# Gate and up projections of a two-layer encoder by Strassen's seven products, gated values kept as float32

## The chip, the cores and the metric

The kernel runs on one core of a Trainium2 chip, in one launch. The metric is the device time of the whole program in microseconds, the median of several executions. The core's engines are TensorE (PE in the rows: matmuls, with weight loads, PEld, beside them), VectorE (DVE), ScalarE (ACT), GpSimd (POOL) and SyncE (SP), whose queue issues all of the large transfers.

## The reference

Two layers over 512 tokens of width 1024, all in float32. Each layer first mixes positions (differential attention, grouped-query attention and a gated MLP over positions, from one input projection, then an output projection and a layer norm) and then applies the FFN that the change is about:

```python
x = layer_norm(ALPHA * x + mix(x), g1, b1)
gate, up = x @ w_gate, x @ w_up          # 1024 -> 2816 each
x = layer_norm(ALPHA * x + (silu(gate) * up) @ w_down, g2, b2)
```

2816 hidden columns are 22 tiles of 128, called j here.

## The kernel before

Every float32 operand is split into a high part (a cast to the matmul's format, on ScalarE) and a low part (the value minus the cast, on VectorE); `put` (L192 to L195) issues the two. `mm` (L183) then issues three matmuls into one accumulator: high by high, high by low, low by high.

Weights come in pieces of 128 x 1024 float32 (512 KB). `prefetch` walks one list of pieces in the order of use, loads a piece into a raw buffer by a transfer on SyncE, and puts it into two slots of RING (eight slots of 1024 columns, high and low) as soon as two are free; `done` gives slots back. So SyncE's transfers, ScalarE's casts and VectorE's subtractions of the weights run ahead of TensorE as far as slots allow.

The FFN of a layer starts in `main` after the output projection w_out. Per block of 128 tokens (tb) w_out's second half ends with `residual` and `layer_norm` (L298 to L314), and `turn_x` transposes the block's 1024 columns in two banks of PSUM and puts them into xT: two splits of 512 columns per block, of which block 3's are the last.

`gate_up` then runs per tile j: a gate and an up matrix, each 8 slices of 128 of the contraction, each slice `mm` on 512 tokens: 2 x 8 x 3 = 48 matmuls of 512 columns. Tiles 0 and 1 are done in two halves of 256 tokens, the first half while blocks 2 and 3 are still in the output projection's layer norm. `hidden` (L811 to L816) takes silu of the gate on ScalarE, the product with up on VectorE, and puts it into hT, split for the next product. `down` multiplies hT by w_dn, with 22 pieces; its first 16 tiles run in order, the last six (`ntail`) are kept for a pass block by block, so that the layer norms of blocks 0 to 2 lie under TensorE.

GpSimd computes only the layer norms' power (`rsqrt`, L235) in this part. An order within each engine's queue is chosen at build time by a scheduler that follows the program order and the priorities in `PRI`; TensorE's order is that of the generators in `Flow`.

## Time and profile before

| | |
|---|---|
| median of 3 runs | 1199.77 us (1199.49 to 1199.92) |
| profiled execution, its own span | 1198.6 us |
| TensorE busy | 1174.0 us, 98% |
| VectorE busy | 634.3 us, 53% |
| ScalarE busy | 497.5 us, 42% |
| GpSimd busy | 127.6 us, 11% |
| layer 0, gate and up, tiles 0 and 1 in halves | 233.6 to 262.2 us |
| layer 0, gate and up, tiles 2 to 21 | 262.2 to 479.8 us |
| layer 0, down | 479.8 to 599.7 us |
| granted TensorE clock, all 40 slices of the page | 0.9 or more |

The profile covers one execution, so its span is compared with itself and the medians with each other. Times in the timeline are counted from the start of the span. A busy share is a mean over stages: the windows show each stage on its own, and the idle time behind a group of instructions names the engine or the transfer that ended the wait.

### The profile page before, as it was taken

How to read it: one execution, taken by the hardware profiler on the slowest of the kernel's cores; microseconds unless marked ns; L12 is line 12 of the kernel's file. 1: busy time of each engine (PE TensorE's matmuls, PEld its weight loads, DVE VectorE, ACT ScalarE, POOL GpSimd, SP SyncE). 2: the span in 40 equal slices, each digit the busy share in tenths (PEclk: the TensorE clock that was granted, in tenths of full speed). 3: DMA queues.
4: the chain of work that ended last, by engine and by line, in shares of the span. 5: the costliest groups of instructions: out<-in, count | busy, mean ns of one | idle time of the engine just before them, and what ended most of it. 6: DMA issues, size and time to landing. Idle time of an engine off the chain costs nothing.

```text
span 1198.6 us, 14610 instructions
## 1 busy us (share of the span) xinstructions
PE 1174.0 (98%) x5634; PEld 941.8 (79%) x5634; DVE 634.3 (53%) x1084; ACT 497.5 (42%) x1000; POOL 127.6 (11%) x118
## 2 busy tenths in 40 slices
PE   9999989999999999999999999999999999999997
PEld 7787666798888888888878776677988888888886
DVE  5788977843332334230774889788333333333316
ACT  5678856433232323220154788663322232332200
POOL 1233230100000000000231232301000000000001
PEclk9999999999999999999999999999999999999999
DMA  8302130042323233441051022202323232234301
GB/s 290 136 1 89 57 103 1 27 168 88 106 88 106 88 106 106 137 145 53 1 164 52 18 71 85 74 1 84 128 90 103 90 104 93 101 106 151 112 1 71
DMA packets 32757, 107.64 MB, mean 90 GB/s; under 512 B 4656, under 2 KB 5680, under 8 KB 32688
## 3 DMA queue, kind: packets, MB, share of 16 engines
q1 hardware_dynamic: 32688, 106.71, 27.1%
q8 instruction: 44, 0.72, 0.3%
q14 instruction: 25, 0.20, 0.0%
HBM read 104.60 MB, written 2.10 MB: 89 GB/s over the span
## 4 chain that ended last, share of the span: by engine, by line
PE 85%; DVE 8%; issue 2%; ACT 2%; DMA 1%; POOL 1%; POOLq 0%; ACTq 0%
PE bank L78 81%; PE bank L82 5%; DMA RAW<-w_in 1%; POOL st L235 1%; DVE XT L195 1%; DVE st L638 1%; DVE we L753 1%; DVE st L743 1%; DVE qTB L611 0%; DVE we L644 0%; DVE X L314 0%; DVE st L302 0%; DVE X L300 0%; POOL RING L209 0%; DVE RING L195 0%
## 5 line engine op out<-in xcount | busy, mean ns | idle before, releaser
L78 PE MATMUL bank<-XT,RING 128*128 128x512 f32 (+1 forms) x2304 | 484.6, 372 | 0.4 <-DVE RING L195 0.4
L78 PEld LDWEIGHTS bank<-XT,RING 128*128 128x128 f32 x2304 | 407.8, 188 | 75.6 <-DVE RING L195 0.9
L194 ACT CAST RING<-RAW 128x1024 fp32r<-128x1024 f32 (+1 forms) x138 | 143.6, 1041 | 399.2 <-PE bank L78 355.0
L195 DVE TENSOR_TENSOR RING<-RAW,RING 128x1024 fp32r<-128x1024 f32 (+1 forms) x130 | 157.1, 1209 | 199.0 <-ACT RING L194 194.6
L78 PE MATMUL bank<-RING,XT 128*128 128x512 f32 x576 | 158.7, 405 | 0.5 <-DVE XT L195 0.3
L235 POOL TENSOR_TENSOR st<-st 128x1 f32<-128x1 f32 (+2 forms) x44 | 54.1, 1230 | 665.4 <-DVE st L308 531.3
L78 PEld LDWEIGHTS bank<-RING,XT 128*128 128x128 f32 x576 | 106.0, 189 | 23.2 <-ACT RING L194 0.7
L815 DVE TENSOR_TENSOR sg<-sg,bank 128x512 f32<-128x512 f32 x44 | 30.3, 688 | 137.1 <-PE bank L78 135.7
L82 PE MATMUL bank<-ident,we 128*128 128x128 f32 x400 | 62.1, 274 | 6.6 <-DVE va L704 5.0
L82 PEld LDWEIGHTS bank<-ident,we 128*128 128x128 f32 x400 | 48.4, 140 | 23.2 <-ACT XT L194 4.0
L750 ACT ACTIVATE we<-bank,st 128x512 f32<-128x512 f32 x64 | 50.6, 791 | 17.8 <-DVE st L746 16.6
L300 DVE SCALAR_TENSOR_TENSOR X<-X,bank 128x512 f32<-128x512 f32 x32 | 21.9, 683 | 66.9 <-PE bank L78 66.8
L78 PE MATMUL bank<-XT,mixAC 128*128 128x512 f32 x192 | 54.8, 413 | 0.7 <-DVE XT L195 0.7
L743 DVE TENSOR_REDUCE st<-bank 128x1 f32<-128x512 f32 x64 | 43.7, 685 | 14.8 <-PE bank L78 14.2
L639 ACT ACTIVATE we<-bank,st 128x512 f32<-128x512 f32 x64 | 44.3, 698 | 13.0 <-DVE st L638 8.8
L725 ACT COPY we<-bank 128x512 f32<-128x512 f32 x64 | 37.8, 591 | 23.1 <-PE bank L82 23.0
L638 DVE TENSOR_REDUCE st<-bank 128x1 f32<-128x512 f32 x64 | 43.3, 682 | 5.1 <-PE bank L78 4.8
L78 PE MATMUL bank<-kT,qTB 128*128 128x512 f32 x128 | 44.4, 428 | 0.7 <-ACT we L750 0.7
L78 PE MATMUL bank<-we,va 128*64 128x512 f32 x192 | 43.8, 598 | 0.0
L78 PEld LDWEIGHTS bank<-XT,mixAC 128*128 128x128 f32 x192 | 35.6, 194 | 9.0 <-DVE XT L195 1.2
L78 PE MATMUL bank<-RING,mixBr1a 128*128 128x512 f32 x128 | 42.7, 411 | 0.0
L209 POOL TENSOR_TENSOR RING<-RAW,RING 128x512 fp32r<-128x512 f32 x4 | 7.1, 1781 | 311.2 <-ACT RING L207 311.2
(178 smaller groups left out, 1548.8 us busy)
## 6 DMA issues: line engine op xcount, KB each, us to landing
RAW<-w_gu SPq DMA_DIRECT2D x88, 512.0 KB, 3.5
RAW<-w_dn SPq DMA_DIRECT2D x44, 512.0 KB, 3.5
RAW<-w_in SPq DMA_DIRECT2D x28, 512.0 KB, 3.6
RAW<-w_out SPq DMA_DIRECT2D x16, 512.0 KB, 3.6
we<-xT SPq DMA_DIRECT2D x8, 256.0 KB, 5.3
X<-x SPq DMA_DIRECT2D x4, 512.0 KB, 7.1
GB<-ln_g SPq DMA_DIRECT2D x4, 512.0 KB, 4.9
GB<-ln_b SPq DMA_DIRECT2D x4, 512.0 KB, 4.6
```

Source lines behind the costliest of these rows:

```text
L78: self.pin(self.nc.tensor.matmul(out, lhs, rhs, **kw))
L82: self.pin(self.nc.tensor.transpose(out, src, ident))
L194: nc.scalar.copy(out=r(dst[0]), in_=src)
L195: (low or nc.vector).tensor_tensor(out=r(dst[1]), in0=src, in1=dst[0], op=ALU.subtract)
L235: POOL.tensor_tensor(out=out, in0=src, in1=k.mhalf[:, 0:n], op=ALU.pow)
L300: DVE.scalar_tensor_tensor(out=xs, in0=xs, scalar=scale, in1=bank, op0=ALU.mult, op1=ALU.add)
L638: DVE.tensor_reduce(out=nm, in_=S, op=ALU.max, axis=AX.X, negate=True)
L639: ACT.activation(out=e[m], in_=S, func=AF.Exp, bias=nm, accum_out=ss[m])
L725: ACT.copy(out=wT[:, :, c], in_=tbk.rearrange("p (k q) -> p k q", k=NT))
L743: DVE.tensor_reduce(out=nm, in_=S, op=ALU.max, axis=AX.X, negate=True)
L750: ACT.activation(out=p_, in_=S, func=AF.Exp, bias=nb, scale=sc, accum_out=s_)
L815: DVE.tensor_tensor(out=sg, in0=sg, in1=B[bk[1]], op=ALU.mult)
```

## The change

Tokens are cut into two halves (0 to 255, 256 to 511) and the contraction into two halves of 512. With these and the two column blocks gate and up, each tile is a product of 2 x 2 blocks, and Strassen's form (in Winograd's variant) computes it by seven products instead of eight. A product is 4 slices x 3 matmuls of 256 columns, 12 matmuls. `gate_up` runs two tiles at a time, product by product in turn, in the order 1, 7, 6, 2, 5, 4, 3.

The operands are sums. On the token side, `turn_xs` takes for blocks 0 and 1 the two splits as before and a raw copy; for each of blocks 2 and 3 it makes four sums of 512 columns on VectorE and five splits, into seven arrays `blk`. On the weight side, `operand_gu` makes four differences of 128 x 512 per tile on GpSimd; each product's operand is then put into one ring slot, so that eight products can be ahead. The raw weights of a tile are four buffers in rotation.

Products 1 and 2 need only blocks 0 and 1 of the tokens and unchanged gate weights. For the first six tiles (`NEARLY`) they run first, twelve products, with weights loaded for them alone (the gate piece of these tiles is loaded again for the rest). The other products are 10 per pair of tiles for tiles 0 to 5 and 14 for the rest.

`gates` joins the products: sums that share a bank are accumulated there, and between them ScalarE or VectorE copies a bank into another one, or into `m7`, `up2` or `hid`. For a tile of the first six, product 1 is kept in `hid` and copied back into a bank by VectorE before product 6. GpSimd multiplies one half of the gated values (128 x 256), VectorE the other. `hid` stays float32, and is put into slots ("hd" in the list of pieces) in the down stage, beside w_dn; the last six tiles' go where raw weights were. w_out's second half is used in the order 6, 7, 4, 5, and pieces 4 and 5 go where xT was.

```diff
+NEARLY = 6
+PRODUCTS = [(j, i) for n in range(0, NEARLY, 2) for i in (1, 2) for j in (n, n + 1)]
+PRODUCTS += [(j, i) for n in range(0, NF, 2) for i in (1, 7, 6, 2, 5, 4, 3) for j in (n, n + 1)
+             if n >= NEARLY or i not in (1, 2)]
...
+        def diff(n, out, x, y):
+            if n not in t:
+                with pri("wsum"):
+                    ins = POOL.tensor_tensor(out=out, in0=x, in1=y, op=ALU.subtract)
...
+        if i in (1, 2, 3):
+            return (g0, g1, u1)[i - 1]
+        t7 = diff(7, k.wt7[j % 4], u1, u0)
...
+        t5 = diff(5, u0, u0, g0)
...
+        t6 = diff(6, g0, u1, t5)
+        return t6 if i == 6 else diff(4, g1, g1, t6)
...
-            pool_ = spare if key[0] == "dn" and len(spare) >= NS else free
...
+            pools = [more, free] if key[0] in ("gu", "hd", "dn") and pool_ is free else [pool_]
...
+                if n == 1:
+                    parts = [s[0][:, 0:T], s[0][:, T:2 * T]]
+                    k.put(parts, operand_gu(*key[1:]) if key[0] == "gu" else k.hid[key[2]])
...
+            if tb >= 2:
+                with pri("turn_x"):
+                    r22, s1, s2, s3 = (flat(t) for t in k.xsum[tb - 2])
+                    a11, a12 = (k.rawA[i][:, :, cols] for i in range(2))
+                    DVE.tensor_tensor(out=s3, in0=a11, in1=src[0], op=ALU.subtract)
+                    ACT.copy(out=r22, in_=src[1])
+                    k.put(part(7), s3)
+                    DVE.tensor_tensor(out=s1, in0=src[0], in1=r22, op=ALU.add)
+                    DVE.tensor_tensor(out=s2, in0=s1, in1=a11, op=ALU.subtract)
+                    k.put(part(6), s2)
+                    k.put(part(5), s1)
+                    k.put(part(4), src[1])
+                    DVE.tensor_tensor(out=r22, in0=a12, in1=s2, op=ALU.subtract)
+                    k.put(part(3), r22)
...
+        def product(j, i, bank, start):
+            w = need(("gu", l, j, i))
+            for kk in range(4):
+                k.mm(bank[:, HT[0]], [q[:, kk * P:(kk + 1) * P] for q in w], [x[:, kk] for x in k.blk[i]],
+                     start and kk == 0, kk == 3, skip_group_check=True)
...
+                if i == 1:
+                    if j < NEARLY:
+                        ACT.copy(out=h2, in_=p)
+                    else:
+                        ACT.copy(out=q, in_=p)
+                elif i == 2:
+                    ACT.activation(out=h1, in_=p, func=AF.Silu)
+                elif i == 7:
+                    ACT.copy(out=m7, in_=v)
+                    if j < NEARLY:
+                        DVE.tensor_copy(out=q, in_=h2)
+                elif i == 6:
+                    ACT.copy(out=v, in_=q)
+                elif i == 5:
+                    DVE.tensor_tensor(out=up2, in0=v, in1=m7, op=ALU.add)
+                elif i == 4:
+                    DVE.tensor_tensor(out=h2, in0=q, in1=m7, op=ALU.add)
+                    ACT.activation(out=h2, in_=h2, func=AF.Silu)
+                    POOL.tensor_tensor(out=h2, in0=h2, in1=up2, op=ALU.mult)
+                elif i == 3:
+                    DVE.tensor_tensor(out=h1, in0=h1, in1=v, op=ALU.mult)
```

How this moves instructions, at three places of layer 0. In the program's rows L93 is a matmul and L97 a transpose of after (L78 and L82 before), L249 and L250 the cast and the subtraction of `put` (L194 and L195 before), L433 and L434 the layer norm's last two steps (L313 and L314 before), L345 a weight difference.

TensorE before, from the end of w_out into the FFN (`bank_69`, `70`, `74` and `75` hold tiles 0 and 1; `bank_72` and `73` take the transposes of blocks 2 and 3):

```order
L78 MATMUL bank_70<-RING,mixBr1b_1382 128x512
L78 MATMUL bank_69<-XT,RING 128x256
L82 MATMUL bank_72<-ident,X 128x128
L78 MATMUL bank_69<-XT,RING 128x256
L82 MATMUL bank_72<-ident,X 128x128 x3
L78 MATMUL bank_69<-XT,RING 128x256 x11
L78 MATMUL bank_70<-XT,RING 128x256
L82 MATMUL bank_73<-ident,X 128x128 x4
L78 MATMUL bank_69<-XT,RING 128x256 x11
L78 MATMUL bank_70<-XT,RING 128x256 x23
```

and after, from the fifth of the twelve early products to product 6 of tiles 0 and 1 (`blkr` holds token sums):

```order
L97 MATMUL bank_71<-ident,X 128x128 x4
L93 MATMUL bank_74<-XT,RING 128x256 x12
L97 MATMUL bank_76<-ident,X 128x128 x4
...
L93 MATMUL bank_74<-XT,RING 128x256 x12
L93 MATMUL bank_75<-XT,RING 128x256 x12
L93 MATMUL bank_72<-blkr_1598,RING 128x256 x12
L93 MATMUL bank_73<-blkr_1598,RING 128x256 x12
L93 MATMUL bank_69<-blkr_1598,RING 128x256 x12
L93 MATMUL bank_70<-blkr_1598,RING 128x256 x12
```

The twelve early products, in banks 74 and 75 in turn, and products 7 of both tiles stand ahead of product 6 of tile 0, the first into `bank_69`.

VectorE before, from the last layer norm of w_out (block 3) into the first gates:

```order
L313 SCALAR_TENSOR_TENSOR X<-X,st,GB 128x1024
L195 TENSOR_TENSOR RING<-RAW,RING 128x1024 [waits DMAHW5_49,Activation_49]
L314 SCALAR_TENSOR_TENSOR X<-X,st,GB 128x1024 [waits DVE_49,Pool_49]
L195 TENSOR_TENSOR XT<-bank_73,XT 128x4x128 [waits PE_49]
L195 TENSOR_TENSOR RING<-RAW,RING 128x1024 [waits DMAHW6_49,Activation_49]
L195 TENSOR_TENSOR XT<-bank_72,XT 128x4x128 [waits Activation_49]
L195 TENSOR_TENSOR XT<-bank_73,XT 128x4x128 [waits Activation_49]
L195 TENSOR_TENSOR RING<-RAW,RING 128x1024 [waits DMAHW0_49,PE_49,Activation_49]
L815 TENSOR_TENSOR sg_1931<-sg_1931,bank_70 128x512 [waits PE_49,Activation_49]
```

and after, the head and the end of what stands between the same layer norm and the copies of product 1 back into banks 69 and 70 (`xsum` are the token sums, `ffnwe` raw weights and their differences, `ffnqk` is `hid`):

```order
L434 SCALAR_TENSOR_TENSOR X<-X,st,GB 128x1024 [waits DVE_49,Pool_49]
L947 TENSOR_TENSOR xsumkT_1914<-blkraw_1600,bank_72 128x512 [waits PE_49]
L950 TENSOR_TENSOR xsumkT_1914<-bank_72,xsumkT_1914 128x512 [waits Activation_49]
L250 TENSOR_TENSOR RING<-RAW,RING 128x512 [waits DMAHW3_49,PE_49,Activation_49]
L250 TENSOR_TENSOR blkr_1598<-xsumkT_1914,blkr_1598 128x4x128 [waits Activation_49]
L951 TENSOR_TENSOR xsumkT_1914<-xsumkT_1914,blkraw_1600 128x512 [waits DVE_49]
...
L250 TENSOR_TENSOR blkq_1599<-xsumva_1915,blkq_1599 128x4x128 [waits Activation_49]
L250 TENSOR_TENSOR RING<-ffnwe_1823,RING 128x512 [waits DMAHW2_49,PE_49]
L250 TENSOR_TENSOR RING<-ffnwe_1823,RING 128x512 [waits PE_49,Pool_49]
L250 TENSOR_TENSOR RING<-ffnwe_1823,RING 128x512 [waits PE_49,Activation_49] x3
L987 COPY bank_69<-ffnqk_1958 128x256
L987 COPY bank_70<-ffnqk_1958 128x256
```

Between L434 of block 3 and the first L987 stand 32 operations of 512 columns: six that read a bank, 26 with two SBUF inputs.

GpSimd before, from the layer norms of w_out (L235) to those of the layer's end:

```order
L195 TENSOR_TENSOR RING<-RAW,RING 128x1024 x4
L235 TENSOR_TENSOR st<-st 128x1 x4
L209 TENSOR_TENSOR RING<-RAW,RING 128x512
L235 TENSOR_TENSOR st<-st 128x1 x3
L209 TENSOR_TENSOR RING<-RAW,RING 128x512 x3
```

and after, from the same layer norms (now L290) on (`ffnw` is the fourth raw buffer, L995 the multiplication):

```order
L290 TENSOR_TENSOR st<-st 128x1 x4
L345 TENSOR_TENSOR ffnwe_1823<-ffnwe_1823 128x512 x8
L345 TENSOR_TENSOR ffnwe_1823<-RAW 128x512
L345 TENSOR_TENSOR RAW<-RAW 128x512 x3
L345 TENSOR_TENSOR ffnwe_1823<-ffnw_2176 128x512
L345 TENSOR_TENSOR ffnw_2176<-ffnw_2176 128x512 x3
L345 TENSOR_TENSOR ffnwe_1823<-ffnwe_1823 128x512 x8
L995 TENSOR_TENSOR ffnqk_1958<-ffnqk_1958,ffnr1b_2175 128x256 x2
L345 TENSOR_TENSOR ffnwe_1823<-RAW 128x512
```

GpSimd's queue, which held nothing in the FFN but the layer norms, now holds eight differences per pair of tiles (tiles 0 to 5 ahead of the first multiplication).

## Rows read from the trace of the kernel before

**Rows 1.** The page, part 1: engine, busy us, share of the span, instructions.

```profile
PE 1174.0 (98%) x5634; PEld 941.8 (79%) x5634; DVE 634.3 (53%) x1084; ACT 497.5 (42%) x1000; POOL 127.6 (11%) x118
```

**Rows 2.** Windows of layer 0's FFN (columns in its first line).

```profile
core 0: us, PE busy (x) PEld busy (x) DVE busy (x) ACT busy (x) POOL busy (x), PEclk, DMA share, GB/s
233.60:245.00 11.40, 11.19 (x94) 10.95 (x93) 9.96 (x14) 4.42 (x7) 1.52 (x1) 1.00 0.53 179
...
262.20:479.80 217.60, 217.60 (x961) 180.23 (x961) 75.94 (x81) 64.62 (x81) 0.00 (x0) 1.00 0.31 100
479.80:599.70 119.90, 119.90 (x531) 97.58 (x530) 43.51 (x50) 23.15 (x24) 8.41 (x6) 1.00 0.26 84
```

**Rows 3.** Chain of waits, 233 to 340: start, us, what.

```profile
236.77 6.60 PE bank L78 x55
243.83 0.11 PE bank L82
...
245.33 94.84 PE bank L78 x472
```

**Rows 4.** Lines by form, whole run; behind the bar busy us, mean ns.

```profile
L78 PEld LDWEIGHTS bank<-XT,RING 128*128 128x128 f32 x2304 | 407.8, 188 | 75.6 <-DVE RING L195 0.9
L195 DVE TENSOR_TENSOR RING<-RAW,RING 128x1024 fp32r<-128x1024 f32 x126 | 154.3, 1225 | 198.3 <-ACT RING L194 193.9
L194 ACT CAST RING<-RAW 128x1024 fp32r<-128x1024 f32 x134 | 141.1, 1053 | 398.2 <-PE bank L78 355.0 <-DMA RAW<-w_dn 27.8 <-DMA RAW<-w_gu 6.8
L194 ACT CAST RING<-RAW 128x512 fp32r<-128x512 f32 x4 | 2.5, 621 | 1.0 <-DMA RAW<-w_in 0.8
L479 DVE TENSOR_TENSOR rope<-bank,tabs 128x256 f32<-128x256 f32 x16 | 5.9, 412 | 0.8 <-POOL rope L480 0.8
L561 POOL TENSOR_TENSOR GB<-tabs,GB 128x256 f32<-128x256 f32 x4 | 2.9, 735 | 6.7 <-PE bank L78 6.5
```

**Rows 5.** Timeline of GpSimd and VectorE, 27 to 32.6: start, us, engine line op.

```profile
27.33 1.29 POOL L480 TENSOR_TENSOR rope<-rope 128x512 f32<-128x512 f32 x1 [5.50 <-DVE rope L479]
29.49 2.21 POOL L480 TENSOR_TENSOR rope<-rope 128x512 f32<-128x512 f32 x1 [0.87 <-DVE rope L479]
29.33 1.21 DVE L195 TENSOR_TENSOR earlyva<-RAW,earlyva 128x1024 fp32r<-128x1024 f32 x1
30.46 2.38 DVE L352 TENSOR_TENSOR nat<-rope,nat 128x512 fp32r<-128x512 f32 x2
```

**Rows 6.** Timeline of the same two engines at the end of layer 0.

```profile
597.61 0.69 DVE L209 TENSOR_TENSOR RING<-RAW,RING 128x512 fp32r<-128x512 f32 x1
598.56 1.46 DVE L209 TENSOR_TENSOR RING<-RAW,RING 128x512 fp32r<-128x512 f32 x1 [0.26 <-ACT RING L207]
597.66 3.50 POOL L209 TENSOR_TENSOR RING<-RAW,RING 128x512 fp32r<-128x512 f32 x2 [3.44 <-ACT RING L207]
```

**Rows 7.** Timeline of VectorE and GpSimd at the FFN's start.

```profile
238.32 1.52 POOL L235 TENSOR_TENSOR st<-st 128x1 f32<-128x1 f32 x1 [7.54 <-DVE st L308]
240.50 1.28 DVE L314 SCALAR_TENSOR_TENSOR X<-X,st,GB 128x1024 f32<-128x1024 f32 x1
241.69 0.68 DVE L195 TENSOR_TENSOR XT<-bank,XT 128x512 fp32r<-128x512 f32 x1
242.29 1.21 DVE L195 TENSOR_TENSOR RING<-RAW,RING 128x1024 fp32r<-128x1024 f32 x1
```

**Rows 8.** TensorE after a rest: its timeline, and the window behind it.

```profile
159.03 0.63 PE L82 MATMUL bank<-ident,rope 128*128 128x128 f32 x4 [3.08 <-ACT we L725]
160.20:163.60 3.40, 3.40 (x10) 2.63 (x9) 2.07 (x3) 2.66 (x4) 2.30 (x1) 0.50 0.08 25
```

**Rows 9.** Timeline of TensorE where layer 1 begins.

```profile
601.01 0.73 PE L78 MATMUL bank<-RING,XT 128*128 128x512 f32 x2 [0.24 <-ACT XT L194]
```

More of the change, by code (lines that the diff above doesn't have):

```diff
@@ L289, in done @@
     def done(key):
-        _, s, pool_ = held.pop(key)
-        if pool_ is spare or pool_ is free:
-            pool_.extend(s)
+        _, s, homes = held.pop(key)
+        for b, x in zip(s, homes):
+            if x is free or x is more:
+                x.append(b)
         prefetch()
@@ L337, in build @@
             s = [free.pop(0) for _ in range(NS)]
[L338 removed]
+            held[key] = (s, s, [free] * NS)
             nxt[0] += 1
@@ new lines, in turn_xs @@
+        def turn_xs(tb, banks, name):
+            yield LAT["ln"]
+            if tb == 2:
+                yield ev("pv b", NT - 1)
+                k.start_sums(l)
+            cols = slice((tb % 2) * P, (tb % 2 + 1) * P)
+            part = lambda i: [a[:, :, cols] for a in k.blk[i]]
+            flat = lambda t: t.rearrange("p (c t) -> p c t", c=4)
+            src = [flat(banks[hf]) for hf in range(2)]
+            for hf in range(2):
+                with pri("turn_x"):
+                    transposes(banks[hf], lambda c: X[:, tb, (hf * 4 + c) * P:(hf * 4 + c + 1) * P])
+                    if tb < 2:
+                        ACT.copy(out=k.rawA[hf][:, :, cols], in_=src[hf])
+                        k.put(part(1 + hf), src[hf])
+                if hf == 0:
+                    yield 0.0
+            if tb >= 2:
+                with pri("turn_x"):
+                    r22, s1, s2, s3 = (flat(t) for t in k.xsum[tb - 2])
[10 more added lines that the diff above has]
+                    k.put(part(3), r22)
+            F.mark(name, LAT["put"])
@@ new lines, in gate_up @@
+        def gate_up():
+            k.start_ffn(l)
+            got = 0
+            for j, i in PRODUCTS:
+                while got < 4 and not (j < NEARLY and i in (1, 2) and got >= 2):
+                    yield ev("y", got)
+                    got += 1
+                    if got == 4:
+                        k.start_ffn2(l)
+                        k.start_weights2(l)
+                        ready["weights"] = (l, 2)
+                        prefetch()
+                if j < NEARLY and i in (1, 2):
+                    p = (5, 6)[j % 2]
+                else:
+                    p = ((5, 6), (2, 7))[j // 2 % 2][j % 2]
+                bk = (p, (0, 1)[j % 2], (3, 4)[j % 2])
+                bank = B[bk[{1: 0, 2: 0, 6: 1, 4: 1, 7: 2, 5: 2, 3: 2}[i]]]
+                yield from product(j, i, bank, i in (1, 7))
+                gates(j, i, bank, bk)
+                yield 0.0
+            for tag in ("qk1q", "qk1k"):
+                more.extend(k.slots(tag, f"slot{tag}{l}", 2))
+            hfree.extend(k.slots("we", f"slotw{l}", 6))
+            prefetch()
@@ L828, in ffn @@
-            yield ev("y", 1)
-            for j in range(2):
-                yield from gate_up(j, pairs[j % 4], early)
-            yield ev("y", 2)
-            yield ev("y", 3)
-            for j in range(2):
-                yield from gate_up(j, pairs[j % 4], late)
-                hidden(j, pairs[j % 4])
-            for j in range(2, NF):
-                yield from gate_up(j, pairs[j % 4], slice(0, T))
-                hidden(j, pairs[j % 4])
-            dbank = [pairs[(NF - 4 + i) % 4] for i in range(4)]
@@ L867, in ffn @@
                         done(("dn", l, j))
-                    spare.clear()
+                        held.pop(("hd", l, j))
+                    more.clear()
+                    hfree.clear()
                 with pri("ln"):
```

182 lines of the change are left out of this document (131 added, 51 removed).

## The prediction

> **What bounds the kernel now.** I read the page's busy shares first, then the stages of one layer's FFN, then the chain of waits, then prices by line and form, and last single windows in which VectorE and GpSimd work at once. TensorE is busy for 1174.0 of 1198.6 us [rows 1], and in the gate and up stage it never rests: from 262.2 to 479.8, twenty tiles of 48 matmuls, 217.60 of 217.60 us [rows 2], 10.88 us per tile or 0.2267 per matmul of 512 columns. The chain there is TensorE alone [rows 3], where a 256-column matmul takes 6.60/55 = 0.120 us. Beside it VectorE works 75.94 us, ScalarE 64.62 and GpSimd nothing [rows 2]. So a matmul taken away is time taken away, as long as the other engines keep up with what is put on them.
>
> **Products removed: the gain.** Per layer the two first tiles, in halves, cost 2 x 96 x 0.120 = 23.04 us and the other twenty 217.60, together 240.64. After, 22 tiles of 7 products of 12 matmuls of 256 columns are 22 x 84 x 0.120 = 221.76. The gain is 18.88 per layer, **37.8 us** for both. The 256-column pace already stands in the trace with one weight load per matmul, so that the doubled number of loads per column is in the price.
>
> **Work added in the steady state (pairs 3 to 10).** A pair of tiles is 28 x 6 x 0.120 = 20.16 us of TensorE. In this time GpSimd has 8 subtractions of 128x512 and 2 multiplications of 128x256, VectorE 14 low parts of 512 columns and 6 gate steps of 256, ScalarE 14 casts and about 10 copies and silus. ScalarE: 14 x 0.62 + 10 x 0.4 = 12.7, covered [rows 4]. GpSimd alone: 8 x 1.29 [rows 5] + 2 x 0.73 [rows 4] = 11.8, covered. VectorE alone: 14 x 0.60 (start to start, 241.69 to 242.29 [rows 7]) + 6 x 0.41 [rows 4] = 10.9, covered. But the two don't run beside each other where both read SBUF. At 29.49 a GpSimd sum takes 2.21 instead of 1.29: VectorE had begun a two-input SBUF subtraction at 29.33 that held until 30.54, and GpSimd ended 31.70 - 30.54 = 1.16 later; VectorE's next pair took 2.38 instead of 1.29, and its first ended 0.54 after GpSimd's end [rows 5]. At 597.66 two GpSimd subtractions beside such work take 3.50, 1.75 each [rows 6]. So an alternation costs 1.15 + 0.60, one after the other. At 27.33 GpSimd needs its lone 1.29 [rows 5].
>
> The six gate steps have one input in PSUM; I count them as free to run beside GpSimd. What excludes each other in a pair is then 8 x 1.15 + 2 x 0.6 + 14 x 0.60 = 18.8 us, 93% of 20.16. I take a loss of 0, with the ring of eight converted products (8 x 1.44 = 11.5 us of TensorE) against jitter. If the six steps are blocked too it is 18.8 + 2.5 = 21.3, a loss of 1.1 per pair. Between 0 and 9 per layer for eight pairs.
>
> The Trainium skill, in "SBUF — State Buffer" (section "🔬 SBUF: two separate sides"), says that VectorE with two SBUF inputs and a GpSimd operation that reads SBUF exclude each other for the whole instruction, whichever starts first. It speaks against a change that puts 88 subtractions per layer on GpSimd beside 154 of VectorE's; the 2.21 us row agrees with it. By its wording the gate steps, with one PSUM input, aren't held, which is the 0 above; without that distinction the price would be the 9.
>
> **Pairs 0 to 2.** Here 10 products per pair are left, 14.4 us, against 10.4 + 10 x 0.60 = 16.4 of shared reading: 2.0 short each, 6 per layer if nothing was done ahead, 0 if the full ring and the GpSimd results made during the wait described next cover it. I take **2 per layer**.
>
> **The front: the new wait.** Before, each block of 128 tokens was turned with two splits of 512 columns. Now blocks 2 and 3 each need four sums and five splits, and product 6 of tile 0 waits for a VectorE copy that reloads its bank from `hid`; it is queued behind 32 VectorE operations of 512 columns that follow the last layer norm. TensorE's side: it starts at 233.6 [rows 2], has 12 early products, 7(0) and 7(1) in front, 14 x 1.44 = 20.16, and 16 transposes of 0.11 [rows 3]: product 6(0) could start at 255.5. VectorE's side: the last normalisation ends at 240.50 + 1.28 = 241.78 [rows 7]; 32 x 0.60 = 19.2, and the copy 0.41: 261.4 with GpSimd silent. GpSimd begins after its rsqrt, 238.32 + 1.52 = 239.84 [rows 7], with the eight subtractions of tiles 0 and 1: 8 x 1.15 = 9.2. Six of the 32 take one input from PSUM and can hide at most 3.6 of it; I take 2.5, since GpSimd isn't always running when they come. 241.78 + 19.2 + 9.2 - 2.5 + 0.41 = 268.1, a wait of **12.6 per layer**, between 5.9 (no exclusion) and 15.1 (nothing hidden). Waits of single early products on ScalarE, whose queue holds the split of block 2's second sum ahead of a bank's silu, lie inside this time: they delay TensorE, but VectorE's queue ends later. What is queued behind the copy is the next puts; they have slots to spare only after it.
>
> TensorE's old rest at the start of the stage, 11.40 - 11.19 = 0.2 us per layer [rows 2], is within the new wait: I subtract 0.4 for both.
>
> **The clock.** TensorE at 159.03 had rested 3.08 us, and from 160.2 to 163.6 the granted clock was 0.50, 1.2 GHz instead of 2.4 [rows 8]: 3.4 us at half pace, 1.7 lost. Inside the front such a drop is hidden by VectorE's lateness; after the last wait it is not. Between 0 and 1.7 per layer; I take **1**.
>
> **Layer change, once.** The last six pieces of w_dn now hold all the ring until the last block, so that w_in's first pieces of layer 1 are split afterwards: a cast of 1.05 and a subtraction of 1.23 [rows 4] where TensorE now resumes at 601.01 after 0.24 us [rows 9]. Between 0 and 4 (four pieces, one after another, partly under matmuls); I take **2**.
>
> **Edits with one answer.** Six gate pieces per layer are loaded twice, 12 x 512 KB: the DMA share in the stage is 0.31 [rows 2], hidden. `hid` is split in the down stage instead of at the gates: the same cast and subtraction, under a stage in which VectorE works 43.51 of 119.90 us [rows 2]. w_out's rows in the order 6, 7, 4, 5 wait for XT: 0 to 1 per layer, 0 taken, the stage's VectorE is busiest there.
>
> **Sum.** -37.8 + 2 x 12.6 - 0.4 + 2 x 2 + 2 x 1 + 2 = -5.0 us. The profiled span is 1198.6 and the median of the runs 1199.77, 1.2 more that lies outside the span and stays: 1199.8 - 5.0 = **1194.8**.
>
> **Rivals.** *Cover holds (B).* The exclusion costs little in the front because GpSimd finds gaps while VectorE waits for transposes and casts: the wait is 5.9, pairs 0 to 2 lose nothing, the clock stays. -37.8 + 11.8 - 0.4 + 2 = -24.4, **1175**. For it: VectorE's queue does stand still for ScalarE at several places; against: both queues are full at exactly 240 to 268, and the rows show no sharing. *The shared read is the bound (C), slower.* The gate steps are held as well, 21.3 per pair: 9 per layer, the front 15.1, pairs 0 to 2 some 4, together 28 per layer: -37.8 + 56.4 - 0.4 + 2 + 2 = +22.2, **1222** at full price. Its place is GpSimd's subtraction beside VectorE's split, and it decides from (37.8 + 0.4 - 4) / 2 = 17.1 us of loss per layer on. For it: 93% is near the end of what can be hidden; against: a pair can use the time TensorE waits in the front to get ahead. *The products don't run at 0.120 (D)*, because loads of 188 ns [rows 4] show through: nothing in rows 3, with the same shapes, says so. At 0.140 per matmul it would be 22 x 84 x 0.020 = 37 per layer more, far slower.
>
> **How the numbers follow.** A as summed 0.47 (1184 to 1203), B 0.25 (1172 to 1184), C 0.25 (1203 to 1222), D 0.03. A measurement of this kernel tells 0.2%, 2.4 us, from no change. Faster by over that (below 1197.4): all of B and 0.33 of A, 0.58. Within: 0.14, the upper part of A. Slower: C and D, 0.28. The range leaves out the lowest of B and the upper half of C with D: 1174 to 1212.
>
> **What would show it.** The stretch of 14-product pairs should show TensorE starting a tile every 10.08 us without rests. The front should show the VectorE copy into a bank near 268 and TensorE waiting for it; if that wait is under 7 us, B; if over 14, or if TensorE waits for VectorE's RING in every pair, C. GpSimd's subtraction should average 1.7 us beside VectorE, and VectorE's put about 1.2 where it meets one. A granted clock of 0.50 after 6(0) confirms the clock's term. Wrong would be: other waits at the head, above all ScalarE's queue standing for VectorE's sums longer than the copy does, or down-stage splits that come late.

## The result: slower by 1.1%, and the profile after

The changed kernel takes 1213.5 us (median of 4 runs, 1210.9 to 1215.3) against 1199.9 before; the ratio is 1.0108 (95% interval 1.0087 to 1.013). The forecast was 1194.8, the range 1174 to 1212. The profiled span grew from 1198.6 to 1210.7 us. One run of e4_wout_order below, 1615.8 us at a granted clock of 0.65, is left out of its time. These are two lines of the page after: busy time, share and instructions of each engine, and the shares of the chain that ended last ("issue" is time for which the profile shows no cause).

```profile
PE 1153.9 (95%) x7026; PEld 985.6 (81%) x7026; DVE 890.7 (74%) x1432; ACT 633.7 (52%) x1420; POOL 439.8 (36%) x338
...
PE 60%; DVE 13%; issue 11%; POOL 8%; ACT 4%; DMA 4%; SPq 0%; POOLq 0%; DVEq 0%; ACTq 0%
```

TensorE's busy time went down by 20 us and its idle time up by 32. GpSimd went from 127.6 to 439.8 us and VectorE from 634.3 to 890.7 (before: [rows 1]). In the chain of the whole run VectorE, GpSimd and "issue" now hold 32%, 11% before; in this stage TensorE then stood alone in the chain ([rows 3]).

TensorE's waits by what ended them (total us, times, longest). L979 is ScalarE's copy of product 1 out of its bank, L987 VectorE's copy back, L997 the last gate step of a tile:

```profile
PE bank L93 <- ACT ffnqk L979: 12.7, 4, 3.9
PE bank L93 <- DVE bank L987: 9.9, 2, 5.3
...
PE bank L93 <- DVE ffnva L997: 1.8, 4, 0.6
PE bank L93 <- DVE ffnkT L997: 1.5, 4, 0.5
PE bank L93 <- DVE ffnr1a L997: 1.0, 2, 0.6
PE bank L93 <- DVE ffnqk L997: 0.8, 2, 0.5
```

12.7 + 9.9 us are the front of both layers, 5.1 us the places between pairs of tiles. These are idle times at one instruction each; what the stage lost in all is in the table below. First the front of layer 0: start, us, engine, line and what released it, for TensorE, GpSimd, ScalarE and VectorE.

```profile
246.41 2.93 PE L93 MATMUL bank<-XT,RING 128*128 128x256 f32 x12 [2.85 <-ACT ffnqk L979]
252.46 9.17 PE L93 MATMUL bank<-XT,RING 128*128 128x256 f32 x60 [3.12 <-ACT ffnqk L979]
...
269.82 3.38 PE L93 MATMUL bank<-blkr,RING 128*128 128x256 f32 x15 [5.34 <-DVE bank L987]
...
236.65 13.28 POOL L345 TENSOR_TENSOR ffnwe<-ffnwe 128x512 f32<-128x512 f32 x8
...
258.44 5.02 POOL L345 TENSOR_TENSOR RAW<-RAW 128x512 f32<-128x512 f32 x3
...
245.47 0.62 ACT L249 CAST blkr<-xsumkT 128x512 fp32r<-128x512 f32 x1 [3.15 <-DVE xsumkT L951]
...
240.22 1.83 DVE L250 TENSOR_TENSOR RING<-RAW,RING 128x512 fp32r<-128x512 f32 x1
...
247.03 0.68 DVE L250 TENSOR_TENSOR XT<-bank,XT 128x512 fp32r<-128x512 f32 x1
...
269.35 0.74 DVE L987 COPY bank<-ffnqk 128x256 f32<-128x256 f32 x2
```

TensorE waits twice for ScalarE (2.85 and 3.12 us), whose queue holds the cast of a token sum (245.47, itself waiting for VectorE) ahead of the copy that would free the bank, and then 5.34 us for the copy at 269.35. GpSimd's eight differences of tiles 0 and 1 take 13.28 us, 1.66 each instead of 1.29 ([rows 5]), and the four of tile 2, of which three are shown, also fall ahead of the copy. VectorE's subtractions beside them take 1.8 us instead of 0.69, while the one that reads a bank (247.03) takes 0.68.

Then the granted clock (the column with 0.50) behind these waits:

```profile
core 0: us, PE busy (x) PEld busy (x) DVE busy (x) ACT busy (x) POOL busy (x), PEclk, DMA share, GB/s
246.40:249.00 2.60, 2.59 (x12) 2.59 (x12) 2.60 (x4) 2.00 (x4) 2.60 (x3) 0.50 0.00 0
252.40:256.00 3.60, 3.54 (x17) 3.54 (x18) 3.49 (x6) 0.95 (x4) 0.00 (x0) 0.53 0.79 274
...
269.80:273.30 3.50, 3.48 (x18) 3.48 (x19) 0.29 (x1) 0.65 (x2) 3.34 (x3) 0.57 0.96 305
273.30:290.00 16.70, 16.55 (x137) 16.14 (x136) 15.76 (x19) 8.99 (x19) 16.15 (x12) 1.00 0.33 115
```

Behind the waits of 2.85, 3.12 and 5.34 us the granted clock was 0.50, 0.53 and 0.57 over 2.6, 3.6 and 3.5 us, that is 1.2 GHz for most of the time, as in [rows 8]; from 273.3 on it was 1.00. In layer 1 the 24 matmuls behind the copy's wait took 5.1 us (872.1 to 877.2, clock 0.52), in layer 0 4.3.

Third, the place where one pair ends and the next begins, near 419 us. GpSimd, ScalarE, VectorE and TensorE in this order:

```profile
413.60 1.29 POOL L345 TENSOR_TENSOR ffnwe<-RAW 128x512 f32<-128x512 f32 x1 [3.35 <-DMA RAW<-w_gu]
...
416.21 1.29 POOL L345 TENSOR_TENSOR ffnwe<-ffnwe 128x512 f32<-128x512 f32 x1
...
417.53 0.62 ACT L249 CAST RING<-ffnwe 128x512 fp32r<-128x512 f32 x1 [4.07 <-POOL ffnwe L345]
...
418.19 1.13 DVE L250 TENSOR_TENSOR RING<-ffnwe,RING 128x512 fp32r<-128x512 f32 x1 [4.13 <-ACT RING L249]
419.23 0.41 DVE L997 TENSOR_TENSOR ffnva<-ffnva,bank 128x256 f32<-128x256 f32 x1
...
419.79 4.42 PE L93 MATMUL bank<-blkr,RING 128*128 128x256 f32 x33 [0.47 <-DVE ffnva L997]
```

The rows read as one chain. GpSimd stands 3.35 us for a weight transfer of the pair after next; the difference that is needed first, at 416.21, is queued behind it. ScalarE's cast waits 4.07 us for that, VectorE's split at 418.19 waits for the cast, and behind it in VectorE's queue stands L997, for which TensorE waits at 419.79 (and, 1.4 us later, a short time more). Pairs start 20.9 us apart, 419.79 and 440.70, where 168 matmuls at 0.120 are 20.16.

Over the whole run, by form, the split of a weight and the difference (the largest group of each):

```profile
L250 DVE TENSOR_TENSOR RING<-ffnwe,RING 128x512 fp32r<-128x512 f32 x172 | 166.5, 983 | 40.1 <-ACT RING L249 35.5
L345 POOL TENSOR_TENSOR ffnwe<-ffnwe 128x512 f32<-128x512 f32 x96 | 146.1, 1530 | 62.6 <-DVE RING L250 36.2 <-DMA ffnwe<-w_gu 24.0
```

These are 0.98 and 1.53 us, where alone they are 0.69 and 1.29.

Outside the stage, TensorE waits three times per layer in w_out's end for ScalarE's and VectorE's evacuations; the kernel before had no such waits there. Two things stand in these queues that did not before: early splits of gate pieces, and GpSimd's splits of the w_out pieces that go where xT was, at 186.24 and 190.56 (2.38 us each; at 161.30 before). Beside the latter VectorE's product of two single columns (L866), 0.15 us elsewhere, takes 1.38 and 1.89 us. What each of the two costs is not separated by a run. The longest wait of layer 0:

```profile
194.81 0.66 PE L97 MATMUL bank<-ident,we 128*128 128x128 f32 x4 [0.85 <-ACT we L845]
```

and at the layer change for pieces of w_in, whose transfer comes late, so that ScalarE's cast waits for it (TensorE, then ScalarE):

```profile
609.77 0.73 PE L93 MATMUL bank<-RING,XT 128*128 128x512 f32 x2 [0.83 <-ACT RING L262]
...
608.67 1.04 ACT L262 CAST RING<-RAW 128x1024 fp32r<-128x1024 f32 x1 [2.39 <-DMA RAW<-w_in]
```

**Where the 12.1 us of the span went.** The gate and up stage runs from its first matmul of 256 columns to its last: 242.85 us per layer before, 246.35 and 246.8 after. (The window that the prediction and the table before it call tiles 2 to 21 starts 3.4 us after the first of their 960 matmuls and reaches 15 matmuls into the down stage. All of them have the same shape and pace, so the price of a tile stands; the stage itself ended at 476.4.) In the changed kernel four of the 16 transposes of blocks 2 and 3 stand before the stage's first matmul, so TensorE's own work up to product 6(0) is 14 x 1.44 + 12 x 0.11 = 21.5 us, from 231.9 to 253.4 in layer 0. The first row is not measured by itself: it is the count of matmuls at the pace of 0.120 us.

| both layers, us | forecast | measured |
|---|---|---|
| products removed | -37.8 | -37.8 |
| start of the stage to product 6(0), above TensorE's own work | +25.2 | +32.8 (269.82 - 253.4, and 16.4 in layer 1) |
| pairs 0 to 2 from there on, without the slow clock | +4.0 | +2.1 |
| the slow clock behind the copy's wait | +2.0 | +3.6 (1.4 and 2.2) |
| pairs 3 to 10, above 8 x 20.16 | 0 | +8.5 (4.2 and 4.3) |
| TensorE's old rest | -0.4 | -0.8 |
| layer change | +2.0 | +3.5 |
| w_out's end (three waits per layer, 3.75 in all, and what they delay) | 0 | +4.0 |
| a wait of 3.1 us in layer 0's attention, with its clock | 0 | -4.1 (0.5 us of it left) |
| the rest | 0 | +0.3 |
| sum | -5.0 | +12.1 |

### The profile page after: what moved, and what is told of

It is laid out like the page before. It is cut to its first block, busy times and chain, and to the rows that moved or that the text cites. A ratio compares the mean times of both kernels' runs of the same rounds, so it can differ in the third digit from the quotient of the medians.

```text
span 1210.7 us, 18861 instructions
## 1 busy us (share of the span) xinstructions
PE 1153.9 (95%) x7026; PEld 985.6 (81%) x7026; DVE 890.7 (74%) x1432; ACT 633.7 (52%) x1420; POOL 439.8 (36%) x338
## 4 chain that ended last, share of the span: by engine, by line
PE 60%; DVE 13%; issue 11%; POOL 8%; ACT 4%; DMA 4%; SPq 0%; POOLq 0%; DVEq 0%; ACTq 0%
PE bank L93 57%; POOL ffnwe L345 4%; PE bank L97 4%; DVE RING L250 3%; DMA RAW<-w_in 2%; ACT RING L249 2%; POOL RAW L345 1%; POOL st L290 1%; DVE st L863 1%; DVE XT L250 1%; POOL ffnw L345 1%; DVE st L758 1%; DMA RAW<-w_out 1%; DMA we<-w_in 0%; DVE we L764 0%
## 5 line engine op out<-in xcount | busy, mean ns | idle before, releaser
L93 PE MATMUL bank<-XT,RING 128*128 128x256 f32 x2112 | 268.4, 287 | 13.1 <-ACT ffnqk L979 12.7
L93 PEld LDWEIGHTS bank<-XT,RING 128*128 128x128 f32 x2112 | 261.9, 195 | 15.1 <-ACT ffnqk L979 14.1
L290 POOL TENSOR_TENSOR st<-st 128x1 f32<-128x1 f32 (+2 forms) x44 | 54.1, 1228 | 440.3 <-DVE st L428 308.0
L250 DVE TENSOR_TENSOR RING<-ffnwe,RING 128x512 fp32r<-128x512 f32 x172 | 166.5, 983 | 40.1 <-ACT RING L249 35.5
L345 POOL TENSOR_TENSOR ffnwe<-ffnwe 128x512 f32<-128x512 f32 x96 | 146.1, 1530 | 62.6 <-DVE RING L250 36.2
L93 PE MATMUL bank<-RING,XT 128*128 128x512 f32 x576 | 159.8, 407 | 2.7 <-DVE RING L264 1.2
L249 ACT CAST RING<-ffnwe 128x512 fp32r<-128x512 f32 x172 | 104.9, 618 | 107.2 <-PE bank L93 73.1
L93 PE MATMUL bank<-blkr,RING 128*128 128x256 f32 x1056 | 137.7, 288 | 15.6 <-DVE bank L987 9.9
L250 DVE TENSOR_TENSOR RING<-RAW,RING 128x512 fp32r<-128x512 f32 (+1 forms) x122 | 130.2, 1073 | 26.8 <-ACT RING L249 17.7
L93 PEld LDWEIGHTS bank<-blkr,RING 128*128 128x128 f32 x1056 | 131.2, 193 | 21.2 <-DVE bank L987 10.3
L249 ACT CAST RING<-RAW 128x512 fp32r<-128x512 f32 (+1 forms) x126 | 94.7, 762 | 73.0 <-PE bank L93 45.7
L93 PEld LDWEIGHTS bank<-RING,XT 128*128 128x128 f32 x576 | 105.8, 189 | 26.2 <-DVE RING L264 1.7
L250 DVE TENSOR_TENSOR RING<-ffnw,RING 128x512 fp32r<-128x512 f32 x56 | 65.5, 1170 | 33.0 <-ACT RING L249 30.3
L93 PE MATMUL bank<-RING 128*128 128x512 f32 x384 | 88.6, 390 | 0.0
L93 PEld LDWEIGHTS bank<-RING 128*128 128x128 f32 x384 | 71.9, 188 | 15.2
L97 PE MATMUL bank<-ident,we 128*128 128x128 f32 x400 | 62.5, 275 | 10.4 <-DVE va L824 5.1
L97 PEld LDWEIGHTS bank<-ident,we 128*128 128x128 f32 x400 | 47.9, 140 | 28.6 <-ACT we L845 7.0
L93 PE MATMUL bank<-blkq,RING 128*128 128x256 f32 x528 | 66.3, 282 | 0.0
L93 PEld LDWEIGHTS bank<-blkq,RING 128*128 128x128 f32 x528 | 64.3, 189 | 0.0
L870 ACT ACTIVATE we<-bank,st 128x512 f32<-128x512 f32 x64 | 50.3, 787 | 12.6 <-DVE st L866 11.9
L249 ACT CAST RING<-ffnw 128x512 fp32r<-128x512 f32 x56 | 34.6, 618 | 42.0 <-POOL ffnw L345 35.9
L345 POOL TENSOR_TENSOR RAW<-RAW 128x512 f32<-128x512 f32 x30 | 45.5, 1518 | 29.1 <-DVE RING L250 28.0
```

The source lines that it names most:

```text
L93: self.pin(self.nc.tensor.matmul(out, lhs, rhs, **kw))
L97: self.pin(self.nc.tensor.transpose(out, src, ident))
L249: nc.scalar.copy(out=r(dst[0]), in_=src)
L250: (low or nc.vector).tensor_tensor(out=r(dst[1]), in0=src, in1=dst[0], op=ALU.subtract)
L290: POOL.tensor_tensor(out=out, in0=src, in1=k.mhalf[:, 0:n], op=ALU.pow)
L345: ins = POOL.tensor_tensor(out=out, in0=x, in1=y, op=ALU.subtract)
```

## The experiments

The theory after the trace: GpSimd's differences and VectorE's splits exclude each other while they read SBUF, and the front and the pairs pay for it. The rival: queue orders are bad (the copy behind VectorE's queue, a difference behind a transfer, ScalarE's evacuations behind token sums), and the shared read is only a bystander. Ratios are to the kernel before.

**e1_no_copyback: without the copy back for tiles 0 and 1.**

```diff
-                    if j < NEARLY:
+                    if 2 <= j < NEARLY:
                         ACT.copy(out=h2, in_=p)
...
-                    if j < NEARLY:
+                    if 2 <= j < NEARLY:
                         DVE.tensor_copy(out=q, in_=h2)
```

> For tiles 0 and 1 product 1 is copied by ScalarE straight into the bank of product 6, so that no VectorE copy stands before it; tiles 2 to 5 as before. Theory (the copy at the end of VectorE's queue is the last wait of the front): product 6(0) starts some 5 us earlier and the drop of the clock after it goes, 6 to 7 us per layer, total near 1200. Rival (VectorE's queue as a whole is late, the copy is only its last member): products 6, 5 and 4 wait for their own operands instead, at most 3 us per layer is won, total 1207 or more.

Measured: 1209.5 us, ratio 1.0087 (1.0068 to 1.0107); 4 us won, not 14: the rival. TensorE's timeline shows where the wait went:

```profile
253.55 9.18 PE L93 MATMUL bank<-XT,RING 128*128 128x256 f32 x60 [4.37 <-ACT ffnqk L979]
...
269.59 1.70 PE L93 MATMUL bank<-XT,RING 128*128 128x256 f32 x12 [1.16 <-ACT bank L989]
273.23 6.07 PE L93 MATMUL bank<-XT,RING 128*128 128x256 f32 x36 [1.95 <-ACT bank L989]
```

Product 6 starts without a wait, but the early products wait longer (4.37) and product 5 waits for a bank copy (1.16 and 1.95), which stands behind casts in ScalarE's queue. The copy was the last link of a late queue, not its cause.

**e2_no_diffs: GpSimd's differences left out.**

```diff
             if n not in t:
+                t[n] = x
+            if n not in t:
                 with pri("wsum"):
```

> GpSimd's 88 weight differences per layer are left out (each product takes one of its two raw halves instead), everything else stands. Theory (GpSimd's and VectorE's shared reading sets the front, and GpSimd's queue the wait at each pair): the copy before product 6(0) comes 8 to 9 us earlier, the wait at the pairs goes (5 us per layer), total 1180 to 1186. Rival (queues of VectorE and ScalarE in a bad order, GpSimd innocent): the front is the same within 3 us per layer, total 1203 or more.

Measured: 1178.1 us, ratio 0.9822 (0.9797 to 0.9846); 35 us less than the changed kernel, even more than the theory gave. The split has its lone price again:

```profile
L250 DVE TENSOR_TENSOR RING<-ffnwe,RING 128x512 fp32r<-128x512 f32 x152 | 104.3, 691 | 56.2 <-ACT RING L249 52.7
```

So the 176 differences of the run cost 35 us, nearly all that the removed products bring. Whether by reading, by GpSimd's time, or by the chain behind them is not told by this run.

**e3_pool_order: all differences in program order on GpSimd.**

```diff
-                    if j < 2:
-                        tc.keep_in_program_order(ins)
+                    tc.keep_in_program_order(ins)
```

> All weight differences stay in the order in which the program names them on GpSimd (in the changed kernel only those of tiles 0 and 1 do), so that none of the next pair but one stands ahead of one that is needed sooner. Theory (TensorE's wait of 0.8 us at each pair comes from a difference that waits on GpSimd for a weight transfer, with one needed sooner queued behind it): the waits at the pairs shrink from 5 to under 1.5 us per layer, total 1204 to 1207. Rival (the shared read is used up): the waits stay, total within 3 us of 1213.

Measured: 1207.8 us, ratio 1.0068 (1.0053 to 1.0083). The total is near what the theory gave, the place only in part. TensorE's timeline, front and steady state:

```profile
266.30 3.11 PE L93 MATMUL bank<-blkr,RING 128*128 128x256 f32 x24 [1.68 <-DVE bank L986]
...
282.04 4.54 PE L93 MATMUL bank<-blkr,RING 128*128 128x256 f32 x36 [1.93 <-DVE ffnqk L996]
...
397.55 5.98 PE L93 MATMUL bank<-blkr,RING 128*128 128x256 f32 x48
...
417.73 5.98 PE L93 MATMUL bank<-blkr,RING 128*128 128x256 f32 x48
```

From pair to pair it is now 20.18 us (397.55 to 417.73), TensorE's own pace: the wait at the pairs came from the order in GpSimd's queue, and the shared read is not used up there. Only the last pair of a layer waits again, 1.2 us in layer 0. The wait for the copy shrank too (1.68): one difference of tile 2 runs ahead of it instead of four, and product 6 starts 3.5 us earlier, 3 x 1.15. But the pairs of tiles 2 to 5 now wait 1.9 us each, and some tenths more, on the last gate step.

**e4_wout_order: w_out's second half as before the change.**

```diff
-BBS, XBB = (6, 7, 4, 5), (4, 5)
+BBS, XBB = (4, 5, 6, 7), ()
```

> The second half of w_out in its old order 4 to 7 and in ring slots, as in the kernel before. Theory (early weight splits among the attention's evacuations on ScalarE cost TensorE 2.4 us in the end of w_out): these waits go, and the early gate pieces come later; total 1208 to 1211. Rival (the early splits are needed that early): what is won in w_out is lost in the front, total 1213 or more.

Measured: 1226.5 us, ratio 1.0222 (1.0197 to 1.0247): 13 us more, the rival and beyond it. The waits in w_out are gone, but the front pays, and the wait in layer 0's attention ([rows 8]) is back (both lines are TensorE's):

```profile
157.94 0.63 PE L97 MATMUL bank<-ident,rope 128*128 128x128 f32 x4 [3.17 <-ACT we L845]
...
277.80 4.71 PE L93 MATMUL bank<-blkr,RING 128*128 128x256 f32 x24 [9.72 <-DVE bank L987]
```

With its slots in the ring later, the first splits come late and the copy comes 8 us later. So w_out's new order and places cost 4.0 us in w_out's end and bring 4.1 in layer 0's attention, beside what the front gains from early slots. The wait in the attention is made by the exclusion as well. In the kernel before, VectorE's timeline has

```profile
155.20 2.31 DVE L746 TENSOR_TENSOR st<-st 128x1 f32<-128x1 f32 x1
```

a product of two single columns that takes 0.14 us at 150.04. Here it stands beside two splits that GpSimd makes for w_out from 152.58 to 157.49, as does the scaling ahead of it (2.08 us instead of 0.48). ScalarE's exponential waits for it, then TensorE. In e4_wout_order the same product takes 2.31 us again; in the changed kernel it stands ahead of that scaling and is done by 154.6.

**e5_diffs_dve: the differences on VectorE.**

```diff
-                    ins = POOL.tensor_tensor(out=out, in0=x, in1=y, op=ALU.subtract)
-                    if j < 2:
-                        tc.keep_in_program_order(ins)
+                    DVE.tensor_tensor(out=out, in0=x, in1=y, op=ALU.subtract)
```

> The 88 weight differences per layer move from GpSimd to VectorE. Theory (what costs is that GpSimd's read holds VectorE for 1.1 us, where VectorE needs 0.60 for the same difference): a pair has 14 splits, 8 differences and 6 gate steps, 8.4 + 4.8 + 2.5 = 15.7 us of 20.16 on VectorE alone, and the front's 40 operations take 24 us instead of 28, so 8 to 16 us are won, total 1197 to 1205. Rival (VectorE is full as it is, or its in-order queue then waits for weight transfers): total 1210 or more.

Measured: 1189.5 us, ratio 0.9907 (0.9886 to 0.9927): 24 us less than the changed kernel and faster than the one before, more than the theory gave. TensorE's longest wait in the front, then the forms:

```profile
262.40 5.11 PE L93 MATMUL bank<-blkr,RING 128*128 128x256 f32 x24 [8.60 <-DVE bank L985]
...
L250 DVE TENSOR_TENSOR RING<-ffnwe,RING 128x512 fp32r<-128x512 f32 x172 | 118.0, 695 | 26.9 <-ACT RING L249 25.8
L345 DVE TENSOR_TENSOR ffnwe<-ffnwe 128x512 f32<-128x512 f32 x96 | 70.6, 740 | 8.5 <-DMA ffnwe<-w_gu 8.1
```

VectorE does more work in the same busy time (885 us; 891 with the differences elsewhere). A difference costs VectorE 0.74 us; on GpSimd it took 1.53 us and made the splits 0.3 us longer on average. ScalarE's evacuations no longer wait long for late sums; one wait of 8.6 us per layer for the copy is left, which stands behind the differences too.

**e6_pool_fill: GpSimd fills the places with a constant.**

```diff
-                    ins = POOL.tensor_tensor(out=out, in0=x, in1=y, op=ALU.subtract)
+                    ins = POOL.memset(out, 0.5)
```

> GpSimd fills each difference's place with a constant instead of computing it: the same places, waits and orders, but nothing is read; the differences are left out. Theory (GpSimd's reading excludes VectorE's): VectorE's splits take 0.69 beside the fills, total within 6 us of the kernel without differences, 1178 to 1185. Rival (the cost is the chain from GpSimd to ScalarE's cast to VectorE's split and the queues behind it): VectorE still waits at the same places, total 1195 or more.

**e9_pool_fill3: three fills for each difference.**

```diff
-                    ins = POOL.tensor_tensor(out=out, in0=x, in1=y, op=ALU.subtract)
-                    if j < 2:
-                        tc.keep_in_program_order(ins)
+                    for _ in range(3):
+                        ins = POOL.memset(out, 0.5)
+                        if j < 2:
+                            tc.keep_in_program_order(ins)
```

> As e6_pool_fill, but three fills of 0.52 us for each difference, 1.57 us of GpSimd where the difference alone takes 1.29: GpSimd is busy for longer than in the changed kernel without contention, and reads nothing; the differences are left out. Theory (the reading is what excludes, not GpSimd's time or the chain behind it): within 6 us of e6_pool_fill, 1174 to 1184. Rival (GpSimd's time on the way from weight to split is what counts, and e6_pool_fill was fast because a fill is short): 1192 or more.

Measured: 1177.7 us (ratio 0.9807, 0.9776 to 0.9839) with one fill, 1180.6 us (0.9835, 0.9807 to 0.9863) with three: the theory in both. The forms with one fill, and with three:

```profile
L250 DVE TENSOR_TENSOR RING<-ffnwe,RING 128x512 fp32r<-128x512 f32 x172 | 117.9, 691 | 64.8 <-ACT RING L249 60.3
L345 POOL MEMSET ffnwe<- 128x512 f32 x116 | 59.1, 525 | 149.8 <-DVE RING L250 106.2 <-DMA ffnwe<-w_gu 19.6 <-ACT ffnqk L983 13.6
```

```profile
L346 POOL MEMSET ffnwe<- 128x512 f32 x348 | 175.0, 526 | 76.4 <-DVE RING L250 48.1 <-DMA ffnwe<-w_gu 13.2 <-PE bank L93 4.9
L250 DVE TENSOR_TENSOR RING<-ffnwe,RING 128x512 fp32r<-128x512 f32 x172 | 119.9, 704 | 66.3 <-ACT RING L249 61.2
```

With three fills GpSimd works about as long as in the changed kernel (148.0 us against 158.1 from 232 to 480), it still stands for transfers (3.14 us at 396.14), and VectorE's split takes 704 ns. The 33 to 36 us therefore need GpSimd's reading beside VectorE's; GpSimd's time and the chain behind it do not cost them without it. In the pairs the reading needs a bad order too: e3_pool_order wins 5.8 us with the reading left in place. The Trainium skill, "SBUF — State Buffer" (section "Who interferes with whom"), says the same of this pair of engines: an operation of VectorE with at most one SBUF input, outside VectorE's two-port modes, does not contend with GpSimd; one with two does, against an operation of GpSimd that reads and not against one that only writes. The traces agree: 0.68 us for the split out of a bank at 247.03 beside a running difference, 1.8 us for the one out of SBUF, 0.69 to 0.70 us beside fills.

**e7_early0: no early products.**

```diff
-NEARLY = 6
+NEARLY = 0
```

> No products run early (NEARLY is 0): all seven products of a pair run in a row and the first wait for all four token blocks. Theory (the twelve early products cover part of the token sums, 17 us of TensorE beside them): the front's wait grows by 6 to 12 us per layer, total 1225 to 1238. Rival (VectorE's queue ends the front anyway and the early products' own splits lengthen it): total 1205 to 1216.

Measured: 1219.3 us, ratio 1.0154 (1.0124 to 1.0183), between the two. TensorE's two waits in the front:

```profile
248.44 2.93 PE L93 MATMUL bank<-XT,RING 128*128 128x256 f32 x12 [7.20 <-ACT bank L981]
257.73 0.80 PE L93 MATMUL bank<-blkr,RING 128*128 128x256 f32 x2 [6.36 <-ACT blkr L249]
```

The twelve early products are worth 5.8 us, 2.9 per layer, of the 17 us that they last. The first wait is for a copy on ScalarE that stands behind casts of GpSimd's differences (247.50, after 1.05 us for L345), the second for the cast of a token sum: the queues of the other engines set the end in both kernels.

**e10_pool_evac: the orders alone, differences on GpSimd.**

```diff
-PRI = {... "strassen": 0, ...}
+PRI = {... "strassen": -60, ...}
...
-                    if j < 2:
-                        tc.keep_in_program_order(ins)
+                    tc.keep_in_program_order(ins)
...
-                    if j < NEARLY:
+                    if 2 <= j < NEARLY:
```

> The orders alone, with the differences left on GpSimd: product 1 of tiles 0 and 1 copied by ScalarE straight into its bank, gate steps with an earlier priority, differences in program order on GpSimd. Theory (order and shared read cost separately; in e8_dve_evac order gave 13 us on top of the move to VectorE): 8 to 13 us less than e3_pool_order, 1195 to 1200, about the kernel before. Rival (with the shared read in force the order is worth nothing, since VectorE's sums come at 1.75 us each): 1204 to 1209.

Measured: 1206.6 us, ratio 1.0053 (1.0038 to 1.0068), the same as e3_pool_order within its spread. TensorE's waits, and the split:

```profile
PE bank L93 <- DVE ffnqk L996: 12.9, 7, 3.9
PE bank L93 <- ACT ffnqk L982: 6.7, 2, 3.6
...
L250 DVE TENSOR_TENSOR RING<-ffnwe,RING 128x512 fp32r<-128x512 f32 x172 | 172.3, 1035 | 36.5 <-ACT RING L249 36.0
```

The copy's wait (3.4 us in e3_pool_order) is gone, and it came back at the last gate step (L996), 12.9 us where e3_pool_order had 9.5. In the front, as long as a split takes 1.0 us, these two edits only chose who waits.

**e11_dve_nocopy: differences on VectorE, without the copy.** The edit is e5_diffs_dve's and e1_no_copyback's together.

> As e5_diffs_dve with the copy before product 6 of tiles 0 and 1 taken away, priorities as in the changed kernel: splits e8_dve_evac in its two parts. Theory (in e5_diffs_dve TensorE's one long wait of 8.8 us per layer is for the copy alone): 5 to 8 us per layer less than e5_diffs_dve, 1174 to 1180, as e8_dve_evac. Rival (the gate steps' priority does it): within 5 us of 1189.

Measured: 1186.4 us, ratio 0.9887 (0.9869 to 0.9905): 3 us less than e5_diffs_dve, the rival. The wait of 8.6 us became waits for later gate steps:

```profile
274.95 5.94 PE L93 MATMUL bank<-blkr,RING 128*128 128x256 f32 x48 [3.25 <-DVE ffnqk L995]
```

**e8_dve_evac: e11_dve_nocopy with the gate steps earlier in the queues.**

```diff
-PRI = {... "strassen": 0, ...}
+PRI = {... "strassen": -60, ...}
```

> As e5_diffs_dve, and product 1 of tiles 0 and 1 is copied by ScalarE straight into its bank (as e1_no_copyback), and the scheduler's priority of the gate steps is 60 earlier, so that ScalarE empties the banks of the early products before it waits for VectorE's token sums. Theory (the three waits of the front are ScalarE's queue behind VectorE's sums, twice, and the copy): 4 to 8 us per layer less than e5_diffs_dve, total 1186 to 1194, faster than the kernel before. Rival (VectorE's sums set the front in any order): within 3 us per layer of e5_diffs_dve.

Measured: 1176.1 us, ratio **0.979** (0.9769 to 0.9811), faster than before by 2.1%, better than expected. What waits are left in the front:

```profile
245.90 6.02 PE L93 MATMUL bank<-XT,RING 128*128 128x256 f32 x48 [1.50 <-ACT ffnqk L981]
...
271.69 4.63 PE L93 MATMUL bank<-blkr,RING 128*128 128x256 f32 x36 [0.69 <-DVE ffnqk L995]
```

The longest is 1.50 us, and the mean granted clock is 1.00 from 245 to 350 us. The gate and up stage takes 228.6 and 228.0 us, 14.6 less per layer than before, of an ideal 18.9. The priority is worth 10 us here on top of e11_dve_nocopy; with the differences on GpSimd the priority and the missing copy together were worth 1 (e10_pool_evac against e3_pool_order).

**e12_tail5: e8_dve_evac with five pieces of w_dn in the last pass.**

```diff
-KNOBS = {... "ntail": 6, ...}
+KNOBS = {... "ntail": 5, ...}
```

> As e8_dve_evac, with the last five pieces of w_dn instead of six kept for the pass block by block, so that two ring slots come free before layer 1's input projection. Theory (TensorE's waits of 3.7 us at the layer change are for pieces of w_in that found no slot): 1 to 3 us less than e8_dve_evac, 1173 to 1175. Rival (the pass no longer covers a block's layer norm and transposes): 1176 to 1182.

Measured: 1173.6 us, ratio 0.9784 (0.9765 to 0.9804), the fastest of all, though its interval overlaps e8_dve_evac's. Instead of several waits for w_in (L264), one is left at the layer change:

```profile
588.41 9.59 PE L93 MATMUL bank<-RING,XT 128*128 128x512 f32 x41 [1.86 <-DVE XT L250]
```

It waits for the last block's transposes (XT), which the shorter pass covers less. Whether 2.4 us were won is not settled by these intervals.

## Why the prediction was wrong

1. **The removed products: right.** 0.120 us per matmul of 256 columns held in the new stage; in e3_pool_order a pair takes 20.18 us.
2. **The exclusion: right in kind, and its unit price too.** I wrote 1.15 + 0.60 per alternation; in the front VectorE's splits took 1.75 to 1.83 us and GpSimd's differences 1.66.
3. **The front, "12.6 per layer": too small, 16.4.** This is the second step that failed. The term that was mis-sized is GpSimd's: I counted the eight differences of tiles 0 and 1, and twelve ran ahead of the copy, since tile 2's weights had landed by 256.7. Four more at 1.15 are 4.6 us. VectorE finished its last layer norm at 236.78 + 2.32 = 239.1, 2.7 us earlier than in [rows 7], and still reached the copy at 269.35, 1.7 us later than I had it: 4.4 us. In e3_pool_order only one difference of tile 2 ran ahead, and product 6 came 3.5 us earlier. (The rest of the 3.8 us is TensorE, ready at 253.4 instead of 255.5.) That the copy itself was to blame is refuted by e1_no_copyback: it was only the last in line.
4. **Pairs 3 to 10, "a loss of 0": wrong, 8.5 us in both layers.** This is the step that failed most. The load was sized well (in e3_pool_order only the last pair of a layer waits), but I looked only at sums of busy time. What I left out is the order within GpSimd's queue: a difference that waits for a transfer stops the ones behind it, and three engines later TensorE. That cost 0.8 to 1.0 us at five of the eight pairs of layer 0, 4.2 us in all, and 4.3 in layer 1; pairs 0 to 2 lost 1.3 and 0.8, less than the 2 that I took.
5. **The clock, "1 per layer":** right in kind, too small: 24 matmuls behind the copy's wait took 4.3 us in layer 0 and 5.1 in layer 1, where 2.9 are their price, so 1.4 and 2.2 were lost; my upper bound was 1.7. The two earlier drops lie inside the front.
6. **w_out, "0 taken": wrong by 4.0 us.** The rows of w_out's end were not priced: I counted the new slots and not the splits that they let in, of gate pieces and of w_out's own on GpSimd, among the attention's evacuations. The layer change cost 3.5 instead of 2, in waits for pieces of w_in; e12_tail5, which frees slots earlier, takes these waits away.
7. **Not foreseen, in the other direction:** layer 0's wait of 3.1 us in the attention ([rows 8]) shrank to 0.5 and the slow clock behind it went, 4.1 us. It belongs to the same edit: in e4_wout_order, with w_out's old order, it is back with 3.17 us. That the total missed the range by no more than 1.5 us is in part this luck.
8. **The rivals.** C named the mechanism and its deciding point, 17.1 us of loss per layer; the stage lost 23 above its ideal length (223.1 with twelve transposes), and the kernel became slower. C's place, gate steps held as well, was not what happened: those ran at 0.41 to 0.43 throughout (L991, L993 and L997 from 300 to 480). What failed, then, is not the exclusion and its price but the sum made with it: four differences too few in the front (item 3), and no term for a delay that one engine's queue hands to the next (items 4 and 6).

The experiments put the size on it. The differences on GpSimd cost 33 to 36 us (e2_no_diffs, e6_pool_fill, e9_pool_fill3), against a gain of 37.8; the same subtractions on VectorE cost 12 us (e5_diffs_dve against e6_pool_fill), and with better orders the kernel that makes them there is as fast (e8_dve_evac) as the kernels that make none in the old orders. What the better orders would win in a kernel without differences was not run, so it is not shown that the differences on VectorE cost nothing.
